# A hand-planned hybrid decoder layer: new order of the front units, new planner prices, new due times of the weight sums

## The chip, the core and the metric

The kernel runs on one core of a Trainium2 chip. Its engines are PE (TensorE: matmuls, transposes, and weight loads, which the profile lists as PEld), DVE (VectorE), ACT (ScalarE), POOL (GpSimd) and SP (SyncE, which issues nearly all DMAs here). Each engine works through its own queue in the order in which the program issued the instructions. The metric is the time of one execution in microseconds (us); lower is better.

## What is computed

One layer with two token mixers side by side on 1024 tokens of width 1024. All data is float32.

```python
h = rms_norm(x, norm_w)
proj = h @ w_in
q, k, v, z_a, xbc, z_s, dt_raw, gate_logits = jnp.split(proj, SPLIT_POINTS, axis=-1)
y_a = diff_attention(q, k, v, ...) * silu(z_a)          # 8 heads, two causal softmax maps each
xbc = silu(causal_depthwise_conv(xbc, conv_w, conv_b))
xs, Bm, Cm = jnp.split(xbc, ...)
y_s = ssd_chunked(xs, softplus(dt_raw + dt_bias), A, Bm, Cm, d_skip)   # 4 groups, chunks of 128 tokens
y_s = gated_group_rms_norm(y_s, z_s, ssd_norm_w)
g_a, g_s = jnp.split(gate_logits, 2, axis=-1)
merged = sigmoid(g_a) * (y_a @ w_proj_attn) + sigmoid(g_s) * (y_s @ w_proj_ssd)
x = x + merged @ w_out
```

## The kernel before

Every large product is made of matmuls on a high and a low part: a float32 operand is copied by ACT into the matmul's reduced format (the high part), and a subtract gives the low part (a "split"); three matmuls (high by high, high by low, low by high) make one block. Large products also use a seven-product scheme on 2 by 2 blocks: sums of blocks, called t1 to t4 ("forms") for the activations, and sums of weight blocks are made first, seven products p = 1 to 7 are run in place of eight, and DVE adds them up.

**The planner.** All instructions are written out by generators under a planner (class `Plan`). It keeps a clock `pl.t`, which moves with each PE instruction by a price, and a busy time for each other engine, which `act`, `tt`, `stt` and their like move by a price worked out from the size. A generator yields the planned time at which its next input will be ready. The planner always resumes whatever is due, so the prices and the due times decide in which order the instructions stand in each engine's queue. They decide nothing else: on the chip an instruction waits for semaphores, however late they come. [...]

**The front**, to about 580 us. `FRONT_ORDER` lists its units, and `bulk` runs them one after the other on PE:

- y0, y1 (`z_first`): plain z units, eight weights of 128x512 each, all of the first four token tiles; y0 starts while the tokens still come in and are normalised.
- e0, e2, e4, e6 (`gate_first`): half of a gate block row in two parts of 12 matmuls. The first part is copied out by ACT (`gc`) before the second part goes on in the same PSUM bank.
- c0 to c22 (`front_pair`): a pair of 128-column blocks of xBC in the seven-product scheme, seven products of 12 matmuls; each of its outputs then runs through the depthwise convolution and silu (`conv`, mostly on DVE).
- g0 to g10 (`front_pair`): the same for gates; those whose e unit came before need five products.
- z03 to z17 (`z_part`): one product p of the seven for z, 48 matmuls; the first digit is the half of the columns. Its weights are plain blocks or, for p = 3, 5, 6, 7, sums that `weight_sums` made.
- d0 (`dt_proj`): the dt projection; `dt_rest` then makes the scan's tables, mostly on DVE.

`form_evac` makes the forms of the second four tiles, t2 first, then t3, t1, t4. A weight set of a c or g unit is made by `pair_splits`: four additions on POOL, up to seven splits on ACT and DVE, some low halves on POOL. Raw weights have 4 buffers, split weights 9, both handed on in the order of the list `wlist`, which follows `FRONT_ORDER`; so the order of the units is also the order of the loads on SP.

**Behind the front** come eight heads (`att_proj` and the attention blocks), with the scan's 32 chunks spread between them (`ssd_core`), then four gate block rows (`gates`), the products with w_proj_ssd and w_proj_attn (`products`) and the last product (`final`). `ssd_core` waits `PACE` of planned time between chunks of a group, or `SLOW` = 32.0 while the front still holds its buffers.

**Weight sums.** `weight_sums(n, ...)` loads blocks of w_in (n = 0, 1) or w_out (n = 2), makes four sums of each four blocks on POOL (16 additions, 16 loads and 16 stores for each n) and stores them in `wf_d`, from which the z units and the last product load them. `ZSUMS` holds the due times. The first two are on the planner's clock; the third is an offset to the clock at the end of the heads.

**WPOOL, NEARLY.** In `w_splits` a 128x512 weight with index i in `wlist` has its low half made on POOL when i is at least `NEARLY`, a multiple of `WPOOL` and not one of the last product's; otherwise DVE makes it.

The prices that the change touches are in `mm`, `act`, `tt` and `stt` (the whole functions follow).

Of the kernel before, what the change touches and what calls it, by code (L numbers as in the profile page):

```python
# [30 lines left out]
C_ZS = 7168  # L31
C_DT = 9216
C_GATE = 9248
NBIG, NW, NRAW, NMID, NSM = 17, 9, 4, 16, 8
PACE = 19.5
FRONT = 12
SLOW = 32.0
FRONT_ORDER = "y0 e6 y1 e0 e4 c6 e2 d0 c20 z06 c16 z07 z05 g0 c2 z04 c0 z16 z03 g2 z17 z15 z14 c4 z13 c8 g8 c14 g6 c22 g10 c12 g4 c10 c18"
REST = (("t2", 6), ("b22", 3), ("t3", 7), ("t1", 5), ("t4", 4))
ZSUMS = (75.0, 182.0, 11.0)  # L40
WPOOL = 3
NEARLY = 48
FINAL = (("b11", 1), ("t1", 5), ("t2", 6), ("t3", 7), ("b21", 2), ("b22", 3), ("t4", 4))
NFIN = 4 * len(FINAL)
HOP = 0.12
# [100 lines left out]
def tile_hybrid_layer(ctx: ExitStack, tc: tile.TileContext, x, norm_w, w_in, q_norm_w, k_norm_w,  # L146
# [4 lines left out]
    w_in, w_pa, w_ps, w_o = w_in[0], w_proj_attn[0], w_proj_ssd[0], w_out[0]  # L151
# [24 lines left out]
    pl = Plan()  # L176
# [10 lines left out]
    def midt(shape=(P, 512), dt=F32, name="m"):  # L187
        return mid.tile(list(shape), dt, tag="b2", name=name)
# [16 lines left out]
    lag = [0.0135, 1.5]  # L205

    def mm(o, lhsT, rhs, start, stop, after=0.0, **kw):
        nc.tensor.matmul(o, lhsT=lhsT, rhs=rhs, start=start, stop=stop, **kw)  # L208
        n, m = rhs.free_size(), lhsT.free_size()
        if rhs.dtype == F32:  # L210
            c = max(4 * n / 2400, 0.215)
        else:
            c = max(n / 2400 + lag[0], 0.057 if m <= 64 else 0.107)
        pl.t = max(pl.t, after) + c

    def tp(o, i, idn=None, after=0.0):
# [11 lines left out]
    def in_ps(*aps):  # L228
        return any(a.space == bass.MemoryType.PSUM for a in aps)
# [3 lines left out]
    def act(o, i, f, after, **kw):  # L233
        nc.scalar.activation(o, i, f, **kw)  # L234
        if f in (AF.Silu, AF.Exp) and f != table[0]:
            table[0] = f
            pl.op("A", 1.3, after)
        c = 0.83e-3 * i.free_size() + (0.052 if in_ps(i) else 0.093) + 0.093 * (("accum_out" in kw) + any(not isinstance(kw.get(i, 0.0), float) for i in ("scale", "bias")))
        return pl.op("A", c, after)

    def tt(o, a, b, op, after, eng="V"):
        (nc.vector if eng == "V" else nc.gpsimd).tensor_tensor(out=o, in0=a, in1=b, op=op)  # L242
        n = o.free_size()
        if eng == "G":
            return pl.op("G", 0.095 + (1.85e-3 if op == ALU.mult else 2.3e-3) * n, after, True)
        sb = not in_ps(a, b)
        return pl.op("V", 0.07 + 0.07 * sb + 1.042e-3 * n, after, sb)

    def stt(o, a, s, b, op0, op1, after):
        nc.vector.scalar_tensor_tensor(out=o, in0=a, scalar=s, in1=b, op0=op0, op1=op1)  # L250
        sb = not in_ps(a, b)
        return pl.op("V", 0.07 + 0.07 * sb + 1.042e-3 * o.free_size() + (0.0 if isinstance(s, float) else 0.06), after, sb)

    def tsc(o, a, s, op, after):
        nc.vector.tensor_scalar(out=o, in0=a, scalar1=s, scalar2=None, op0=op)
# [6 lines left out]
    def load(o, i, after=0.0):  # L262
        nc.sync.dma_start(out=o, in_=i)
        q = pl.op("Q", 0.48, max(after, pl.t))
        n = o.free_size() * 512 / 360e3 if o.space != bass.MemoryType.DRAM else i.free_size() * 512 / 360e3
        return pl.op("D", n, q + 0.6) + lag[1]
# [32 lines left out]
    ready = {}  # L299
# [59 lines left out]
    ORDER1 = []  # L359
    for e in FRONT_ORDER.split():  # L360
        ORDER1.append((e[0], int(e[1:])))
# [88 lines left out]
    def w_splits():  # L450
        for i in range(len(wlist)):
# [20 lines left out]
            if i >= len(wlist) - NFIN:  # L472
                yield from pl.room("V", 2.0)
            t = tt(lo, raw, hi, ALU.subtract, t, "G" if NEARLY <= i < len(wlist) - NFIN and i % WPOOL == 0 else "V")
            raws.give(kr, t)
# [307 lines left out]
    def att_setup():  # L783
        ready['setup'] = 1
        for i in range(2):
            kqlo.append((yield from pl.get(bigs)))
            q = bigt([P, 2, 512], F32R, name=f"qlo{i}")
            nc.gpsimd.memset(q[64:P, 0].bitcast(F32), 0.0)
            nc.gpsimd.memset(q[0:64, 1].bitcast(F32), 0.0)
            qlo.append(q)  # L790
# [549 lines left out]
    def z_part(pr, p, keep):  # L1340
        f, ids = FORM_OF[p], w_next(4)
        for t in range(4):
            k = yield from pl.get(trs, first=True)
            pm = trt(f"pz{p}{pr}{t}")
            if f[0] == "t":
                yield from formed(f, (4 + t,))
            us = {}
            pl.spawn(z_fetch(pr, p, t, us))
            for kb in range(4):
                yield from w_need(ids[kb])  # L1350
                yield from steps3(pm, [a[:, t * P:(t + 1) * P] for a in front_form(f, kb)], wide(ids[kb]), kb == 0, kb == 3)
                if t == 3:
                    w_done(ids[kb])
            pl.spawn(z_step(pr, p, t, pm, k, us, keep), pe_done())
# [117 lines left out]
    def ssd_core(g):  # L1472
# [20 lines left out]
        for c in range(NT):  # L1493
# [4 lines left out]
            pl.spawn(ssd_chunk(g, c, state, abs_))  # L1498
            yield pl.t + (PACE if bigs.avail(3) <= pl.t or 'setup' in ready else SLOW)

# [179 lines left out]
    def gates():  # L1680
        for ob in range(FRONT, 16):
            ids = w_next(2)
            for n in range(2):
                k = yield from pl.get(trs, first=True)
                pm = mmt(f"pg{ob}{n}")
                yield from proj_half(pm, ids, n, n == 1, ob == 15 and n == 1)
                pl.spawn(gate_evac(ob, n, pm, k), pe_done())
# [21 lines left out]
    def prepare():  # L1709
        for c, g in ((0, 1), (1, 3)):  # L1710
            while ready.get("ssd", {}).get(g, INF) > pl.t:
                yield pl.t + 0.5
            yield from sums_of(c, range(4))
            if c == 0:
                pl.spawn(prepare_a())

    def weight_sums(n, src, c0, at=0.0):
        yield at
        for kb in range(4):
            ks = yield from pl.get(mids, 4)  # L1720
            a, b = [[midt(name=f"os{n}{kb}{j}{i}") for i in range(2)] for j in range(2)]
            t = max(load((a, b)[j][i], src[(j * 4 + kb) * P:(j * 4 + kb + 1) * P, c0 + i * 512:c0 + i * 512 + 512])
                    for j in range(2) for i in range(2))
            yield t
            for p, x, k, o, y, z, op in ((5, b[1], 3, b[1], b[1], a[1], ALU.add), (7, a[1], 1, a[1], a[0], a[1], ALU.subtract),
                                         (6, a[0], 0, a[0], b[1], a[0], ALU.subtract), (3, b[0], 2, b[0], b[0], a[0], ALU.subtract)):
                yield from pl.room("G")
                t = tt(o, y, z, op, t, "G")
                pl.spawn(sum_store(n, kb, p, x, ks[k], t))
                if p == 3:  # L1730
                    ready["summed", n, kb] = t
                t -= HOP

    def sum_store(n, kb, p, x, k, t):
        yield t
        j, h = {6: (0, 0), 7: (0, 1), 3: (1, 0), 5: (1, 1)}[p]
        ready[n, kb, p] = t = load(wf_d[n * 4 + kb, j][:, h * 512:(h + 1) * 512], x, t)
        while p == 6 and ("summed", n, kb) not in ready:
            yield pl.t + 0.2
        mids.give(k, max(t, ready["summed", n, kb]) if p == 6 else t)  # L1740
# [389 lines left out]
    def ssd_all():  # L2130
        for g in range(GROUPS):
            while "tables" not in ready:
                yield pl.t + 0.5
            yield from ssd_core(g)

    def bulk():
        pl.spawn(ssd_all())
        pl.spawn(prepare())
        step = {"y": z_first, "h": att_proj, "e": gate_first}
        for i in range(2):  # L2140
            pl.spawn(weight_sums(i, w_in, C_ZS + i * 1024, ZSUMS[i]))
        for n, (kind, i) in enumerate(ORDER1):
            if kind in PAIR_C:
                yield from front_pair(kind, i, (kind, i) == FPAIRS[-1])
            elif kind == "z":
                nk, ni = ORDER1[n + 1]
                yield from z_part(*divmod(i, 10), nk == "z" and ni // 10 == i // 10)
            elif kind in step:
                yield from step[kind](i)
            else:  # L2150
                yield from dt_proj() if kind == "d" else att_setup()
        pl.spawn(fill())
        pl.spawn(weight_sums(2, w_o, 0, pl.t + ZSUMS[2]))
        yield from gates()
        lag[:] = [0.0135, 2.5]
        for c in range(3):
            yield from products(c)
        yield from final()
# [38 lines left out]
    with tc.manual_schedule():  # L2197
        pl.spawn(start())
        pl.spawn(rest())
        pl.run(bulk())  # L2200
# [28 lines left out]
```

## Time and profile before

| what | value |
| --- | --- |
| three runs | 1579.36, 1580.61, 1582.21 us; median 1580.61 |
| the profiled execution | 1580.41 us, its span 1578.7 us |
| mean granted PE clock | 0.998 |
| heads' projection `pma` on PE | 581.3 to 1205.1 us |
| gate rows `pg` on PE | 1206.0 to 1264.6 us |
| DMA | 287.38 MB, mean 182 GB/s |

The span runs from the first to the last instruction of the profiled execution. The profile's page gives the busy time of each engine; the view of waits says for each engine how long it stood idle, and which instruction of which engine (or which DMA) ended that. Names are the program's own without buffer numbers: `fYc<-ft,wp` is a matmul into the bank fY of a c unit from a form and a split weight, `pz` a z unit, `pmz` a y unit, `pe` an e unit, `pO`, `px`, `py` banks of the scan (the last two also of the products), `pma` and `sc` a head's projection and scores. `L242` is line 242, the helper `tt`; as most instructions are issued by a helper, the tile's name says more than the line.

### The profile page before, as it was taken

How to read it: one execution, taken by the hardware profiler on the slowest of the kernel's cores; microseconds unless marked ns; L12 is line 12 of the kernel's file. 1: busy time of each engine (PE TensorE's matmuls, PEld its weight loads, DVE VectorE, ACT ScalarE, POOL GpSimd, SP SyncE). 2: the span in 40 equal slices, each digit the busy share in tenths (PEclk: the TensorE clock that was granted, in tenths of full speed). 3: DMA queues.
4: the chain of work that ended last, by engine and by line, in shares of the span. 5: the costliest groups of instructions: out<-in, count | busy, mean ns of one | idle time of the engine just before them, and what ended most of it. 6: DMA issues, size and time to landing. Idle time of an engine off the chain costs nothing.

```text
span 1578.7 us, 24834 instructions
## 1 busy us (share of the span) xinstructions
PE 1553.7 (98%) x7858; PEld 1299.0 (82%) x7858; DVE 1183.6 (75%) x2143; ACT 939.4 (60%) x2273; POOL 785.3 (50%) x906
## 2 busy tenths in 40 slices
PE   7999999999999999999999999999999999999999
PEld 5777888888888888888888888888888888888887
DVE  6778867568787778767778787877556687898985
ACT  7653434467565576778677777776666554443350
POOL 3274465345555554546574846454756745332005
PEclk9999999999999999999999999999999999999999
DMA  6576698744454552424373522333336697798846
GB/s 227 162 250 194 230 301 284 247 153 139 133 150 157 151 158 96 134 62 122 111 236 122 152 89 81 110 112 118 107 134 224 193 366 253 267 323 273 302 140 220
DMA packets 254821, 287.38 MB, mean 182 GB/s; under 512 B 18391, under 2 KB 162528, under 8 KB 254690
## 3 DMA queue, kind: packets, MB, share of 16 engines
q1 hardware_dynamic: 254686, 285.79, 55.7%
q8 instruction: 62, 1.02, 0.3%
q14 instruction: 69, 0.57, 0.1%
q10 hardware_dynamic: 4, 0.00, 0.0%
HBM read 196.47 MB, written 89.26 MB: 181 GB/s over the span
## 4 chain that ended last, share of the span: by engine, by line
PE 85%; ACT 3%; DVE 3%; DMA 3%; POOL 3%; issue 2%; SPq 0%; POOLq 0%; DVEq 0%; ACTq 0%
PE pma L208 19%; PE pz L208 11%; PE py L208 5%; PE fYc L208 5%; PE sc L208 4%; PE pO L208 4%; PE av L208 4%; PE fXc L208 3%; PE fZc L208 3%; PE px L208 3%; PE fYg L208 3%; PE pg L208 2%; PE pmz L208 2%; PE pa L217 2%; PE poz L208 1%
## 5 line engine op out<-in xcount | busy, mean ns | idle before, releaser
L208 PE MATMUL pma<-w,hH 128*128 128x512 f32 x1024 | 343.8, 404 | 0.0
L208 PEld LDWEIGHTS pma<-w,hH 128*128 128x128 f32 x1024 | 187.7, 189 | 32.9 <-DVE xdt L242 0.2
L208 PE MATMUL pma<-w,hL 128*128 128x512 f32 x512 | 205.7, 402 | 0.0
L234 ACT ACTIVATE w<-raw 128x512 fp32r<-128x512 f32 (+1 forms) x166 | 101.3, 629 | 56.0 <-DMA raw<-wf_d 21.7
L242 DVE TENSOR_TENSOR w<-raw,w 128x512 fp32r<-128x512 f32 (+1 forms) x134 | 107.1, 817 | 27.0 <-ACT w L234 24.1
L234 ACT ACTIVATE p<-p,nm 128x256 f32<-128x256 f32 (+7 forms) x128 | 98.8, 774 | 33.8 <-DVE nm L916 33.3
L208 PEld LDWEIGHTS pma<-w,hL 128*128 128x128 f32 x512 | 96.5, 188 | 16.6
L242 POOL TENSOR_TENSOR rawf<-rawf,rawf 128x512 f32<-128x512 f32 x54 | 71.8, 1330 | 75.1 <-DVE wp L242 30.5
L208 PE MATMUL fYc<-ft,wp 128*128 128x512 f32 x432 | 106.5, 392 | 2.4 <-DVE ft L242 1.8
L208 PEld LDWEIGHTS fYc<-ft,wp 128*128 128x128 f32 x432 | 80.3, 188 | 20.2 <-DVE ft L242 2.2
L208 PE MATMUL pz<-w,ft 128*128 128x512 f32 x384 | 90.1, 391 | 0.9 <-DVE w L242 0.9
L234 ACT ACTIVATE wp<-rawp 128x512 fp32r<-128x512 f32 x72 | 44.1, 627 | 78.4 <-POOL rawp L242 25.6
L242 POOL TENSOR_TENSOR os<-os,os 128x512 f32<-128x512 f32 x48 | 66.9, 1393 | 36.4 <-DMA os<-in_w_in_dram 14.8
L208 PEld LDWEIGHTS pz<-w,ft 128*128 128x128 f32 x384 | 71.7, 188 | 16.0 <-DVE w L242 1.3
L242 POOL TENSOR_TENSOR rawp<-rawp,rawp 128x512 f32<-128x512 f32 x36 | 54.4, 1521 | 54.2 <-DVE wp L242 50.2
L234 ACT ACTIVATE ab<-ab,nac 128x128 f32<-128x128 f32 x256 | 78.5, 397 | 3.5 <-POOL ab L1482 3.4
L916 DVE CUSTOM_DVE_ANT_0 p<-sc,maskb 128x512 f32<-128x512 f32 (+3 forms) x128 | 72.4, 584 | 6.6 <-PE sc L208 6.0
L274 POOL TENSOR_TENSOR rs<-rs,mhalf 128x4 f32<-128x4 f32 (+1 forms) x71 | 72.8, 1025 | 5.9
L208 PE MATMUL av<-v,at 128*128 128x128 f32 x576 | 75.2, 275 | 0.0
L208 PEld LDWEIGHTS av<-v,at 128*128 128x128 f32 x576 | 72.5, 191 | 3.2
L234 ACT ACTIVATE wp<-rawf 128x512 fp32r<-128x512 f32 x100 | 60.5, 624 | 17.5 <-POOL rawf L242 16.3
L948 POOL TENSOR_TENSOR rec<-s,mone 128x1 f32<-128x1 f32 x64 | 37.2, 583 | 63.7 <-ACT p L234 62.5
(376 smaller groups left out, 4410.3 us busy)
## 6 DMA issues: line engine op xcount, KB each, us to landing
raw<-in_w_in_dram SPq DMA_DIRECT2D x104, 256.0 KB, 3.2
rawf<-in_w_in_dram SPq DMA_DIRECT2D x72, 256.0 KB, 4.7
ab<-act_d SPq DMA_DIRECT2D x32, 512.0 KB, 4.7
wf_d<-os SPq DMA_DIRECT2D x48, 256.0 KB, 5.1
cv_d<-cv SPq DMA_DIRECT2D x48, 256.0 KB, 2.9
raw<-wf_d SPq DMA_DIRECT2D x48, 256.0 KB, 3.3
t_d<-ts SPq DMA_DIRECT2D x24, 512.0 KB, 4.0
os<-in_w_in_dram SPq DMA_DIRECT2D x32, 256.0 KB, 3.8
```

The costliest lines, as they stand in the source:

```text
L208: nc.tensor.matmul(o, lhsT=lhsT, rhs=rhs, start=start, stop=stop, **kw)
L217: nc.tensor.transpose(out=o, in_=i, identity=ident if idn is None else idn)
L234: nc.scalar.activation(o, i, f, **kw)
L242: (nc.vector if eng == "V" else nc.gpsimd).tensor_tensor(out=o, in0=a, in1=b, op=op)
L274: nc.gpsimd.tensor_tensor(out=dst, in0=dst, in1=mhalf[:, 0:cols], op=ALU.pow)
L916: nc.vector.tensor_tensor_reduce(out=p[:, j:e], in0=sc[i][:, 0:e - j], in1=maskb[:, S - n + j:S - n + e], scale=-1.0, scalar=nms[i - 1] if ...
L948: nc.gpsimd.tensor_tensor(out=rec, in0=sums[1], in1=mone, op=ALU.pow)
```

## The change

It changes the unit order, five constants and some planner prices, and spawns the third weight sums with the first two. No instruction of the computation is added or left out.

```diff
-PACE = 19.5
+PACE = 18.0
-FRONT_ORDER = "y0 e6 y1 e0 e4 c6 e2 d0 c20 z06 c16 z07 z05 g0 c2 z04 c0 z16 z03 g2 z17 z15 z14 c4 z13 c8 g8 c14 g6 c22 g10 c12 g4 c10 c18"
+FRONT_ORDER = "y0 y1 e6 e4 c6 e0 e2 d0 c4 c20 z06 c16 z07 z05 c22 c2 z03 z04 g0 z16 c0 g2 z17 z15 c12 g6 g8 g10 z14 c8 c14 z13 g4 c18 c10"
-ZSUMS = (75.0, 182.0, 11.0)
-WPOOL = 3
-NEARLY = 48
+ZSUMS = (75.0, 187.0, 1190.0)
+WPOOL = 4
+NEARLY = 57
...
-            c = max(n / 2400 + lag[0], 0.057 if m <= 64 else 0.107)
+            c = max(n / 2400 + lag[0], 0.057 if m <= 64 else 0.107) + (0.006 if 'setup' in ready and n == 512 and lag[1] < 2 else 0.0)
...
-        return pl.op("A", c, after)
+        return pl.op("A", c + part(o), after)
+
+    def part(o):
+        return 0.12 if o.shape[0] == 64 else 0.0
...
-        return pl.op("V", 0.07 + 0.07 * sb + 1.042e-3 * n, after, sb)
+        return pl.op("V", 0.065 + part(o) + 1.042e-3 * n, after, sb)
...
-        return pl.op("V", 0.07 + 0.07 * sb + 1.042e-3 * o.free_size() + (0.0 if isinstance(s, float) else 0.06), after, sb)
+        return pl.op("V", 0.065 + part(o) + 1.042e-3 * o.free_size() + (0.0 if isinstance(s, float) else 0.06), after, sb)
...
-        for i in range(2):
-            pl.spawn(weight_sums(i, w_in, C_ZS + i * 1024, ZSUMS[i]))
+        for i, (src, c0) in enumerate(((w_in, C_ZS), (w_in, C_ZS + 1024), (w_o, 0))):
+            pl.spawn(weight_sums(i, src, c0, ZSUMS[i]))
...
         pl.spawn(fill())
-        pl.spawn(weight_sums(2, w_o, 0, pl.t + ZSUMS[2]))
```

`'setup' in ready` holds from the end of the front on; `lag[1] < 2` holds until the gate rows are done. `sb` is true when no input lies in PSUM. `part` is for pieces of 64 partitions, which the heads' q and k stacking uses.

## The prediction

> **What bounds the kernel now.** I read the page first: which engine has no time left.
>
> ```profile
> span 1578.7 us, 24834 instructions
> PE 1553.7 (98%) x7858; PEld 1299.0 (82%) x7858; DVE 1183.6 (75%) x2143; ACT 939.4 (60%) x2273; POOL 785.3 (50%) x906
> ```
>
> PE (TensorE) is busy for 1553.7 of 1578.7 us, so PE's own work is the bound, and the change adds and removes none: it sorts the same units anew. All that can be won is idle time of PE, so the second view is the waits of engine PE alone (who ended the wait; us in total, times, longest).
>
> ```profile
> PE pmz L208 <- ACT zc L234: 4.3, 2, 2.9
> PE pe L208 <- ACT gc L234: 2.9, 4, 0.7
> PE nwb L208 <- POOL one L2164: 2.7, 1, 2.7
> PE fYc L208 <- DVE ft L242: 1.8, 1, 1.8
> PE ph L217 <- DVE x L250: 1.6, 1, 1.6
> PE pO L208 <- POOL wp L242: 1.4, 1, 1.4
> PE py L208 <- DVE u L242: 1.1, 1, 1.1
> PE fXc L208 <- ACT fc L234: 0.9, 1, 0.9
> PE pz L208 <- DVE w L242: 0.9, 1, 0.9
> PE fYg L208 <- DVE fu L242: 0.8, 1, 0.8
> PE fYc L208 <- DVE fu L242: 0.7, 1, 0.7
> PE pod L208 <- DVE xr L250: 0.6, 1, 0.6
> PE pa L217 <- DVE p L250: 0.4, 1, 0.4
> ...
> PE sc L208 <- DVE kk L242: 0.2, 1, 0.2
> ```
>
> The sum is some 22 us; the seven waits from `pa` to the last one are 0.2 to 0.4 each, 2.0 together. Third, the busy times by stage say where they lie (columns: PE, weight loads, DVE, ACT, POOL busy us, then clock, DMA share, GB/s).
>
> ```profile
> 40.00:160.00 120.00, 113.82 (x503) 89.12 (x502) 94.39 (x154) 61.15 (x124) 56.02 (x43) 1.00 0.63 200
> 160.00:440.00 280.00, 280.00 (x1291) 232.63 (x1290) 200.26 (x308) 147.43 (x280) 141.09 (x115) 1.00 0.67 215
> 440.00:580.00 140.00, 136.95 (x661) 113.83 (x660) 106.79 (x165) 85.91 (x170) 76.18 (x68) 1.00 0.48 146
> 580.00:1060.00 480.00, 478.23 (x2783) 411.84 (x2782) 367.78 (x817) 354.56 (x1053) 261.59 (x408) 1.00 0.39 121
> 1206.00:1300.00 94.00, 92.91 (x463) 77.35 (x462) 72.21 (x107) 57.02 (x123) 58.51 (x55) 1.00 0.86 290
> ```
>
> PE idles 6.2 us in 40 to 160 (the four `pe` waits, 1.8 of `ft`, 0.9 of `pz`, 0.7 of `fYc`), nothing in 160 to 440, 3.1 in 440 to 580 (`pO`, `fXc`, `fYg`), 1.8 in 580 to 1060 and 1.1 in 1206 to 1300 (`py`). The front is nearly full already.
>
> **What the change cannot reach.** `nwb` 2.7, `ph` 1.6 and `pmz` 4.3 lie before 40 us, where y0 runs as before; `pod` 0.6 is the last store. The `pe` waits, 2.9, are inside each of the four e units: its second half waits for the copy of its first, and there are still four. The 0.7 of `fYc` follows d0, behind which a c unit still stands. Together 12.8. Left are 1.8 + 1.4 + 1.1 + 0.9 + 0.9 + 0.8 = 6.9, and the 2.0 of the small ones.
>
> **Part 1, the order of the front.** First y1 directly behind y0. Its supply decides (chain of waits and DVE's timeline):
>
> ```profile
> 46.99 2.73 PE pe L208 x12
> 53.41 21.76 PE pmz L208 x96
> 50.90 0.69 DVE L242 TENSOR_TENSOR w<-raw,w 128x512 fp32r<-128x512 f32 x1 [0.89 <-ACT w L234]
> 103.93 2.35 PE L208 MATMUL fYc<-ft,wp 128*128 128x512 f32 x9 [1.76 <-DVE ft L242]
> 102.78 1.42 DVE L242 TENSOR_TENSOR ft<-r,ft 128x256 fp32r<-128x256 f32 x4
> 85.48 2.56 ACT L234 ACTIVATE ft<-r 128x256 fp32r<-128x256 f32 x8
> ```
>
> y1 would start at 47.0 in place of 53.4. Its eight loads pass e6's two on SP's queue, and its splits on ACT and DVE pass them too. With e6's two splits behind them y1's last two move up by two places, and I read the row at 50.90 as the place of the last. PE uses that weight after half of the first tile pair (21.76 / 4 = 5.4) and three blocks of 0.7, near 54.5. No wait, cost 0; were it late, 0.7 for each split that it is late by.
>
> c6 then starts at 47.0 + 21.8 + two e units of 6.4 (53.41 - 46.99) = 81.6, 6.4 us sooner than behind three e units. Its wait of 1.8 is for the form t4: ACT had it copied by 88.0 (85.48 + 2.56), but DVE wrote the low halves in pieces, the last from 102.8 to 104.2. c6 now needs t4 at 103.93 - 1.76 - 6.4 = 95.8. With the pieces done right behind ACT's copy it is ready near 90 and 1.8 goes; if they stay where they are, 6.4 more are lost. I take the first, by the ACT row, which is nearer to the data. `pz` 0.9: the only z unit in 40 to 160 is z06, and it waits for a split on DVE, where I read c20's convolutions in front of it; they run late because d0's table chain shares DVE. Now c4 stands between d0 and c20, so I take it as gone (0 to -0.9). Sum: -2.7.
>
> In 440 to 580 all three waits fall in one unbroken run of ten c and g units (c8 to c18). The new order cuts it by z14 and z13 into runs of four, two and three; but c4 c20 and c22 c2 now touch where the old order had z units. Of the 3.1 I take half, -1.5 (0 to -3.1), and for the new joints one wait of the mean size, 6.9 / 6 = +1.2 (0 to +1.4 at each of the two: +2.8).
>
> **Part 2, the planner's prices.** They move no instruction by themselves, but the planner sorts every queue by them.
>
> ```profile
> 57.88 1.29 DVE L242 TENSOR_TENSOR b<-b,r 128x512 f32<-128x512 f32 x2
> 59.09 1.28 DVE L242 TENSOR_TENSOR r<-b,r 128x512 f32<-128x512 f32 x2
> 622.14 1.41 DVE L242 TENSOR_TENSOR kk<-pq,kk 64x512 fp32r<-64x512 f32 x2
> 182.75 1.90 SPq L263 DMA_DIRECT2D os<-in_w_in_dram  x4
> ```
>
> Two DVE operations with both inputs in SBUF start 59.09 - 57.88 = 1.21 us after the pair before, 0.60 each. The old price is 0.14 + 0.53 = 0.67, the new one 0.60: right. A half-height `kk` takes 1.41 - 0.69 = 0.72; the old price is 0.60, the new one 0.72: right. The second weight sums, due at 182.0 of the planner's clock, left SP at 182.75: in the front that clock holds already, so a better order in the plan should be one on the chip. In the heads I give the corrected prices 0.5 of the 2.0 small waits (0 to -2.0; as much the other way, since the old 0.07 was also a margin).
>
> [...]
>
> ```profile
> L242 DVE TENSOR_TENSOR w<-raw,w 128x512 fp32r<-128x512 f32 x132 | 106.6, 825 | 27.0 <-ACT w L234 24.1 <-POOL xn L242 1.3 <-issue 1.2
> L242 DVE TENSOR_TENSOR hL<-ph,hH 128x512 fp32r<-128x512 f32 x16 | 10.5, 684 | 4.5 <-ACT b L234 4.5
> L242 POOL TENSOR_TENSOR w<-raw,w x32: 1275/1294/1837, 249.1 to 1213.1; 128x512 fp32r<-128x512 f32 x32
> ```
>
> With both inputs in SBUF the same shape takes 825 ns on the mean, with one in PSUM 684. [...]
>
> **Part 3, WPOOL and NEARLY.** Every fourth weight from 57 on, not every third from 48, has its low half made on POOL. By the list's order that is 20 (indices 60, 64, 72, 80 and sixteen of the heads'), 12 fewer than the 32 of the row: POOL loses 12 x 1.3 = 16 us, DVE gains 12 x 0.83 = 10. DVE is 77% busy in the heads (367.78 of 480), so other work of PE hides it: 0 (up to +0.4, one small wait).
>
> **Part 4, PACE 18.0 and the third sums.**
>
> ```profile
> L1482 POOL TENSOR_SCALAR_AFFINE_SELECT ab<-ab x32: 1090/1098/1555, 294.6 to 1064.4; 128x1024 f32<-128x1024 f32 x32
> L208 PE MATMUL pma<-w,hH 128*128 128x512 f32 x1024 | 343.8, 404 | 0.0
> L208 PE MATMUL pma<-w,hL 128*128 128x512 f32 x512 | 205.7, 402 | 0.0
> 1214.39 3.51 SPq L263 DMA_DIRECT2D os<-in_w_out_dram  x4
> 1277.04 5.11 DMA wf_d<-os
> ```
>
> The scan's 32 chunks run from 294.6 to 1064.4, the later ones paced. In the front they are 32 apart, so nine start before 580 and 23 behind it; with 1.5 less for each the scan ends about 35 us sooner, but PE is full there and DVE at 77%: 0 (up to +0.4 for each chunk whose work DVE then does late, one small wait, 9 in all). The extra 0.006 us for each of 1536 matmuls puts the planner's clock 9.2 us later at the end of the heads. The w_out sums were due 11 after that end and left SP at 1214.39; due at 1190 they leave between 0 and 24 us sooner, with 16 loads, 16 stores and 16 additions, past the gate weights on SP and among the last heads' small POOL work. The `py` wait, 1.1, stands at the end of the busiest DMA stretch (share 0.86), whose chain holds such a store: half goes, -0.5 (-1.1 to +0.4).
>
> **The sum.** -2.7 - 1.5 + 1.2 - 0.5 - 0.5 = -4.0. The profiled execution took 1580.4 (1.7 outside the span), the median of the three is 1580.6, so one sum serves both: 1580.4 - 4.0 = **1576.4**.
>
> **Rivals.** *The waits only change places.* Each of the six comes back at a new joint: 1580.4. For it: the front already has 280 us without one, so any new order risks more there than it can win. Against: every wait has its own cause above, and the new order touches most. *Nearly all of it goes*: 6.9 of waits and some of the 2.0: 1580.4 - 7.5 = 1573. For it: the clock of the plan holds at 182. Against: three of the waits were in an order that the same planner made. *Slower: POOL behind c4 and c20.* c4 and c20 now run while POOL makes the first w_in sums; a pair's weight set that misses its turn costs the 1.4 of `pO <- POOL wp`. From six of the 14 sets on (6 x 1.4 = 8.4 against 1576.4) the kernel ends at 1584.8, slower. Against: POOL is 47% busy in 40 to 160 (56.02 of 120) and gets one pair more.
>
> **Chances.** Forecast (1574.5 to 1578.5) 0.45; nearly all goes 0.17; waits change places (1578.5 to 1583.8) 0.23; slower 0.15. About 0.2%, 3.2 us, is what a measurement of this kernel can tell from no change. Faster than 1577.4: three quarters of the forecast and the second case, 0.51; slower than 1583.8: 0.15; between: 0.34. For eight in ten the range goes from 1572 (the second case and a little) to 1584 (the third case whole).
>
> **What would show it.** In the waits of PE: `fYc <- ft` and `pz <- w` gone; `pe <- gc` four times 0.7; the three of 440 to 580 halved. y1 behind y0 without a wait, c6 from about 81. If c6 waits for `ft` by more than 2 us, or new waits on `wp` stand between 120 and 160, part 1 is wrong; if the waits of 580 to 1060 grow beyond 4 us, parts 2 to 4 are.

## The result: 1595.5 us, slower, and the profile after

The changed kernel takes 1595.52 us (median of four runs, 1595.29 to 1596.22) beside 1580.59 of the kernel before (median of four): the ratio is 1.0095, with a 95% interval from 1.0077 to 1.0112. It is 15 us slower where 4 us less were forecast, and outside the range. The profiled execution took 1596.22 us.

The page after, its span and the busy times of the engines:

```profile
span 1594.5 us, 24858 instructions
PE 1560.8 (98%) x7858; PEld 1300.1 (82%) x7858; DVE 1196.2 (75%) x2153; ACT 934.8 (59%) x2269; POOL 772.5 (48%) x896
```

PE has the same 7858 instructions. It idles 33.7 us (before 25.0), and it is busy 7.1 us longer for the same work, so some matmuls run slower; 8.7 and 7.1 make the 15.8 us by which the span has grown. The waits of PE after:

```profile
PE fYg L208 <- DVE fu L245: 4.7, 3, 3.0
PE pmz L208 <- ACT zc L234: 4.3, 2, 2.9
PE pO L208 <- ACT yt L234: 3.6, 1, 3.6
PE pe L208 <- ACT gc L234: 2.9, 4, 0.7
PE nwb L208 <- POOL one L2166: 2.7, 1, 2.7
PE pya L217 <- DVE y L253: 2.2, 2, 1.6
PE pa L217 <- ACT yt L234: 1.7, 1, 1.7
PE ph L217 <- DVE x L253: 1.5, 1, 1.5
PE pa L217 <- DVE y L253: 1.3, 1, 1.3
PE py L217 <- ACT xn L234: 1.0, 2, 0.8
PE sc L208 <- DVE kk L245: 0.9, 1, 0.9
PE pa L217 <- ACT at L234: 0.7, 1, 0.7
```

The waits called out of reach (`pmz`, `pe`, `nwb`, `ph`) are there to within a tenth. `fYc` on `ft`, `pz` on `w`, `pO` on `wp`, `fXc` on `fc` and `py` on `u` are gone. `fYg` on `fu` has grown from 0.8 to 4.7, and new, or longer than before, is a row of waits on `yt`, `y`, `kk` and `at`. The busy times by stage say where (columns as before):

```profile
40.00:160.00 120.00, 117.06 (x516) 91.98 (x517) 97.26 (x149) 63.68 (x128) 61.86 (x46) 1.00 0.58 184
160.00:440.00 280.00, 275.77 (x1237) 227.38 (x1236) 201.16 (x310) 132.19 (x247) 131.63 (x104) 0.99 0.68 218
440.00:580.00 140.00, 138.44 (x662) 114.44 (x662) 104.12 (x169) 90.29 (x180) 70.52 (x64) 1.00 0.58 176
580.00:1060.00 480.00, 470.94 (x2731) 402.54 (x2730) 359.95 (x789) 344.32 (x1018) 253.82 (x391) 1.00 0.38 116
1206.00:1300.00 94.00, 90.75 (x462) 75.29 (x461) 72.95 (x105) 58.20 (x141) 65.10 (x67) 1.00 0.76 265
```

Idle time of PE falls from 6.2 to 2.9 us in 40 to 160 and from 3.1 to 1.6 in 440 to 580: there the change does what was forecast. It rises from 0 to 4.2 in 160 to 440, from 1.8 to 9.1 in 580 to 1060, and from 1.1 to 3.2 in 1206 to 1300. In 160 to 440 the mean clock is also below 1.00. Two stretches make the difference:

```profile
283.10:290.00 6.90, 6.09 (x14) 4.79 (x15) 2.55 (x4) 0.00 (x0) 2.55 (x2) 0.51 0.60 174
870.20:873.60 3.40, 3.40 (x10) 2.62 (x9) 1.01 (x2) 1.53 (x4) 0.66 (x2) 0.50 0.54 169
```

In these 10.3 us the granted clock was half; in the trace of the kernel before every 2 us between 31 and 1575 us has a mean clock of 1.00. By my estimate (half of 10.3, less the idle part) they are some 5 of the 7.1 us that PE is busy longer. Both stand at a long wait, and these come next.

**The place in 160 to 440** is the unit g0. Its third product waits for the sum `fu` (PE's timeline):

```profile
280.54 0.39 PE L208 MATMUL fXg<-hH,wp 128*128 128x512 f32 x1
283.91 5.46 PE L208 MATMUL fYg<-ft,wp 128*128 128x512 f32 x12 [2.99 <-DVE fu L245]
```

Twelve matmuls that take 2.88 to 3.00 us elsewhere in this trace (292 to 440) take 5.46 behind the wait, at a clock of 0.51. The place costs 3.0 and some 2.5 us.

**The longest wait in the heads** is `pO <- yt`. ACT's timeline shows what the small `yt` stood behind, and PE's what waited for it:

```profile
864.31 2.44 ACT L234 ACTIVATE ab<-ab,nac 128x128 f32<-128x128 f32 x8
866.65 2.76 ACT L234 ACTIVATE qh<-pq,cols 64x512 fp32r<-64x512 f32 x4
869.43 0.37 ACT L234 ACTIVATE yt<-pya,cols 128x128 f32<-128x128 f32 x1
...
869.85 0.50 PE L208 MATMUL pO<-sh,ch 128*128 128x512 f32 x1 [3.55 <-ACT yt L234]
```

`pO` doesn't use `yt` at all. It is a product of the scan; `yt` reads `pya`, a transpose of the attention. What they share is a PSUM bank: in the compiled program `pO` was given the bank that `pya` had. That became the main theory.

To compare kernels whose stages have different lengths, I also sum over each stage what every PE instruction takes from its start to the next start, less the median of its shape: the time that PE **loses**. The stages end at the first `pdt`, at the first and the last `pma`, at the last `pg`, and at the end. The first stage, up to `pdt`, scatters by 4 us among the runs of kernels whose order there is the same; it is left out. Each row is one profiled execution; the one of a_slot took 1590.53 us, the longest of its five.

| time lost by PE, us | front behind d0 | heads | gates | rest | sum |
| --- | --- | --- | --- | --- | --- |
| before | 7.9 | 12.4 | 0.9 | 2.3 | 23.5 |
| after | 12.4 | 22.4 | 4.7 | 0.9 | 40.4 |
| after, planner's banks (a_slot) | 12.0 | 15.3 | 3.8 | 1.0 | 32.1 |
| after, w_out sums as before (a_third) | 10.7 | 23.6 | 0.9 | 3.0 | 38.2 |
| after, second sums due at 190 (a_zs190) | 6.4 | 21.7 | 0.7 | 4.1 | 32.9 |
| after, banks and w_out sums (a_slotthird) | 10.8 | 15.3 | 0.9 | 2.9 | 29.9 |
| after, all three (a_zsslot3) | 6.9 | 17.6 | 0.8 | 3.2 | 28.5 |
| after, banks and c0 moved up (a_slotc0) | 11.0 | 15.8 | 3.8 | 0.7 | 31.3 |

### The profile page after: what moved, and what is told of

It reads as the page before. It is cut to its first block, busy times and chain, and to the rows that moved or that the text cites. A ratio compares the mean times of both kernels' runs of the same rounds, so it can differ in the third digit from the quotient of the medians.

```text
span 1594.5 us, 24858 instructions
## 1 busy us (share of the span) xinstructions
PE 1560.8 (98%) x7858; PEld 1300.1 (82%) x7858; DVE 1196.2 (75%) x2153; ACT 934.8 (59%) x2269; POOL 772.5 (48%) x896
## 4 chain that ended last, share of the span: by engine, by line
PE 78%; DVE 6%; ACT 5%; DMA 5%; issue 3%; POOL 1%; SPq 1%; DVEq 0%; ACTq 0%; POOLq 0%
PE pma L208 19%; PE pz L208 8%; PE py L208 6%; PE fYc L208 5%; PE pO L208 4%; PE px L208 4%; PE av L208 3%; PE sc L208 3%; PE fXc L208 3%; PE fZc L208 3%; PE fYg L208 3%; PE pmz L208 2%; PE pa L217 2%; PE fZg L208 1%; PE poy L208 1%
## 5 line engine op out<-in xcount | busy, mean ns | idle before, releaser
L245 DVE TENSOR_TENSOR w<-raw,w 128x512 fp32r<-128x512 f32 (+1 forms) x144 | 120.5, 850 | 16.7 <-ACT w L234 16.0
L208 PE MATMUL sc<-kk,qh 128*128 128x512 f32 (+3 forms) x192 | 66.1, 349 | 0.9 <-DVE kk L245 0.9
```

## Experiments

Every time stands beside runs of the kernel before on the same chip; the ratio is to those, with its 95% interval. Differences in us are ratios times 1581.

### Banks

The planner's `Slots` hands out the bank that comes free first on its clock. The program does not know this choice: `ps_tr` gives a new tile a free bank by its own order. In the changed kernel's compiled program 865 of 897 tiles got, of the banks free at that point of the program, the one whose last reader stands first in it (864 of 897 in the kernel before). `yt` had been issued early, behind a long queue on ACT; so its bank was handed on early although it came free late. The experiment gives each tile the bank that the planner chose. The order of the instructions on every engine stays the same.

```diff
-    def trt(name):
-        return ps_tr.tile([P, 512], F32, tag="tr", name=name)
+    def trt(name, k):
+        return ps_tr.tile([P, 512], F32, tag=f"tr{k}", name=name, bufs=1)
...
-            pO = trt(f"pO{g}{c}")
+            pO = trt(f"pO{g}{c}", k)
```

> The changed kernel, with every PSUM tile put into the bank that the planner's clock chose for it; the order of the instructions on every engine is the same. Theory 1 (banks): in the heads PE waits because the next tile gets the bank whose last reader was issued first, not the one that came free first; of the waits of 580 to 1060 some 8.9 us are of that kind (pa on y 1.4, pa on yt 1.9, pa on at 0.8, pO on yt 3.7), so they go and the time is 7 to 9 us shorter, near 1587.5. Rival (queues): ACT and DVE are late as such under the new pace and prices, and PE waits for their data; then the time stays within 2 us of 1595.5 and the waits come back on data.

Measured: 1586.57 us, 1.0037 (1.0024 to 1.0050); the changed kernel has 1.0095, so 9 us are gone. The waits of PE from 580 to 1206 (there were 9.1 us in eight such rows):

```profile
PE pa L217 <- DVE y L253: 1.3, 1, 1.3
PE py L217 <- ACT xn L234: 0.9, 2, 0.7
PE px L217 <- DVE qlo L253: 0.5, 1, 0.5
PE pa L217 <- DVE p L253: 0.5, 1, 0.5
PE pma L208 <- DVE qk L245: 0.2, 1, 0.2
```

The waits on `yt` and `at` are gone, and the sum fell to 3.4 us; the wait on `y` stays, because there the planner hands on the bank of the same tile. This settles it: ACT was not late as such. Theory 1 holds for most of the heads.

The same edit in the kernel before:

> The kernel before with its PSUM tiles in the planner's banks. Theory 1: only 1.9 us of its waits in the heads are handed-on banks, so 1 to 2 us shorter, 1579. Rival (queues): no change, 1580.6.

Measured: 1583.55 us, 1.0010 (1.0000 to 1.0021). No gain, where theory 1 asked for 1 to 2 us: the waits of 580 to 1206 sum to 1.8 us in the trace, before to 2.0, and short waits came elsewhere (0.6 us of `ph` at 42, 0.7 of `px` at 298). Putting the banks right gains only where the hand-out had gone wrong.

### What holds g0

The load of `fc`, which `fu` needs, left SP at 277.5 behind stores of z04. First it was issued from ACT's queue.

```diff
-            cell["ct"] = load(cell["c"], gc_d[b * P:(b + 1) * P], g_c[kind, b])
+            cell["ct"] = load(cell["c"], gc_d[b * P:(b + 1) * P], g_c[kind, b], nc.scalar)
```

> The changed kernel with the loads of fc (four of them, at g0, g2, g4, g6) issued from ACT's queue in place of SP's; nothing else is moved. Theory 1 (g0 behind z04): the 3.15 us at 280.5 come from that load, issued at 277.5 behind z04's stores on SP's queue, and another 2.7 us from the matmuls at 0.43 us behind the wait; both go, and half of the 2.1 us at g2 and g4: 6 to 7 us shorter, 1589. Rival: DVE's own queue is late at 283; then the wait moves to the next thing and less than 1.5 us go.

Measured: 1596.92 us, 1.0102 (1.0089 to 1.0115). Nothing gained; the load left at 270.1 and the wait was still 3.25:

```profile
281.54 4.57 PE L208 MATMUL fYg<-ft,wp 128*128 128x512 f32 x12 [3.25 <-DVE fu L245]
```

The theory of the load falls here, the rival holds: on DVE `fu` stood right behind weight splits that were late themselves.

```profile
279.44 1.35 DVE L245 TENSOR_TENSOR w<-raw,w 128x512 fp32r<-128x512 f32 x2 [1.26 <-ACT w L234]
280.72 0.68 DVE L245 TENSOR_TENSOR fu<-fc,fYg 128x512 f32<-128x512 f32 x1
```

> Both edits in the changed kernel. If they are independent, the gains add: 13 to 16 us shorter, 1580 to 1582, level with the kernel before; if the planner's promise holds (its clock, in the old prices, ends 7.7 us before that of the kernel before), as far as 1575.

Measured: 1589.07 us, 1.0051 (1.0037 to 1.0064). No gain over the banks alone. In its profile g0's wait was 1.5 us and the slow matmuls were missing (twelve took 3.00), but that was one execution; the times say nothing of it.

The late splits wait for raw weights from `wf_d`, which stood on SP behind stores of z units. So the stores that ACT's own results need went to ACT's queue: `z_d` alone, then `cv_d`, `gt_d` and `gc_d` as well.

```diff
-        at = load(z_d[g, t * P:(t + 1) * P, :], zz, at)
+        at = load(z_d[g, t * P:(t + 1) * P, :], zz, at, nc.scalar)
```

> The changed kernel with its PSUM tiles in the planner's banks (1586.6) and, besides, the z_d stores issued from ACT's queue, which writes zu, in place of SP's. Theory 1b (g0): the load of fc was not the cause, DVE is held by weight splits whose raw loads from wf_d leave SP at 273 to 277, behind z_d stores that wait 5.1 us for ACT; without these stores on SP the raw loads leave some 4 us sooner, the 2.4 us at g0 and the 1.7 us of slow matmuls behind it go: 4 us shorter, 1582.5. Rival: the DMA engines are full there (the share is 0.9 from 262 to 284), the loads come no sooner, and less than 1.5 us go.

> As the run with z_d, and the stores of cv_d, gt_d and gc_d, which ACT writes too, go by ACT's queue as well. Theory 1b: SP waits 76.8 us for cv and 19.5 for fu in the changed kernel; without these its loads run ahead and the waits at g2 and g4 shrink too: 5 to 7 us shorter than with banks alone, 1580 to 1582. Rival (DMA full): as with z_d alone, less than 1.5 us.

> The same four kinds of store by ACT's queue in the kernel before, its banks as they were. Its front has 11 us of waits on data, of which fYg and fXc on fu and fc, pO on wp, pz on w some 5 us could be late loads: 1 to 3 us shorter, 1578; if SP's queue costs nothing there, 1580.6.

Measured: 1588.40 us, 1.0047 (1.0035 to 1.0060); 1595.00, 1.0080 (1.0066 to 1.0093); 1581.66, 0.9999 (0.9990 to 1.0008). No gain, a loss of 7 us, and no difference. In the profile of the first g0's wait was still 3.14 us: SP waiting in its queue for these stores is not what holds g0. If the bytes themselves were (DMA share 0.95 in 260 to 280), half of two kinds of store should show it. This kernel leaves out half of z and of the convolutions:

```diff
-        at = load(z_d[g, t * P:(t + 1) * P, :], zz, at)
+        nc.sync.dma_start(out=z_d[g, t * P:t * P + 64, :], in_=zz[0:64])
...
+    def load2(o, i):
+        nc.sync.dma_start(out=o[0:64], in_=i[0:64])
+        nc.sync.dma_start(out=o[64:128], in_=i[0:64])
...
-        t_z = load(zc, z_d[g, cs, :])
+        t_z = load2(zc, z_d[g, cs, :])
```

> The changed kernel with its PSUM tiles in the planner's banks (1586.6), and half the bytes of two kinds of store: only 64 of the 128 rows of each tile of z_d and cv_d are stored, and the scan reads these rows twice (so half of the gate z and of the convolutions is left out of what is computed). In 220 to 285 this takes 17 stores x 128 KB, some 2.2 MB, 7 us of DMA at the 0.32 MB/us of 260 to 280. Theory 1c (the DMA engines are full before g0, share 0.95): the weights come sooner, the wait of 2.4 to 3.3 us for fu at 283 and the slow matmuls behind it go, and some of the 3 us at 520: 4 to 7 us shorter, 1580 to 1582. Rival (the order of a queue, not the bytes): the wait stays above 2 us, 1586.

Measured: 1591.48 us, 1.0063 (1.0050 to 1.0076), more than with banks alone. g0's wait was 1.58 us in its profile, less but not gone; the scan's four extra loads for each chunk may have taken the rest back. It leans to the bytes and settles nothing.

Then one constant, the due time of the second w_in sums, which the change had set from 182 to 187:

```diff
-ZSUMS = (75.0, 187.0, 1190.0)
+ZSUMS = (75.0, 190.0, 1190.0)
```

> The changed kernel with one constant moved: the second w_in sums due at 190 in place of 187. My prediction treated such a due time as worth nothing by itself: 1595.5. Theory 3 (the plan is a greedy sort that jumps; the change's constants sit on one of its low points): the planner's clock ends 13.1 us later: 1605 to 1609.

Measured: 1587.40 us, 1.0038 (1.0025 to 1.0052): 9 us shorter, where the planner's clock said 13 longer and my prediction nothing. g0 has no wait, twelve of its matmuls take 3.00 us, and the mean clock of the profiled execution is 0.998, as before the change, where the changed kernel has 0.996:

```profile
278.87 0.39 PE L208 MATMUL fXg<-hH,wp 128*128 128x512 f32 x1
279.36 3.00 PE L208 MATMUL fYg<-ft,wp 128*128 128x512 f32 x12
```

SP's queue shows what goes with it. With 187 the last four loads of these sums leave at 244.8, and all that follows leaves late:

```profile
244.82 1.85 SPq L266 DMA_DIRECT2D os<-in_w_in_dram  x4
...
256.93 2.23 SPq L266 DMA_DIRECT2D rawf<-in_w_in_dram  x4
...
273.10 0.38 SPq L266 DMA_DIRECT2D raw<-wf_d  x1
```

With 190 the sums' last loads leave earlier, and g0's weights with them:

```profile
239.14 1.94 SPq L266 DMA_DIRECT2D os<-in_w_in_dram  x4
...
252.59 2.23 SPq L266 DMA_DIRECT2D rawf<-in_w_in_dram  x4
...
267.47 0.37 SPq L266 DMA_DIRECT2D raw<-wf_d  x1
```

A later due time let the loads run earlier: the planner's sort put the sums at another place among the other loads. In the table the front loses 6.4 us in place of 12.4, less than before the change.

### The w_out sums

Their due time alone, back behind the end of the heads; all up to 1190 stays.

```diff
-        for i, (src, c0) in enumerate(((w_in, C_ZS), (w_in, C_ZS + 1024), (w_o, 0))):
-            pl.spawn(weight_sums(i, src, c0, ZSUMS[i]))
+        for i in range(2):
+            pl.spawn(weight_sums(i, w_in, C_ZS + i * 1024, ZSUMS[i]))
...
+        pl.spawn(weight_sums(2, w_o, 0, pl.t + 11.0))
```

> The changed kernel with the third weight sums (w_out) spawned as before, 11 us behind the end of the heads; everything up to 1190 is the same. My prediction: the new due time is worth 0.5 us (py 1.1), so 1596. Theory 2: the earlier loads crowd DVE and the DMA engines in 1206 to 1300, whose waits grew from 1.3 to 3.6: then 2 us shorter, 1593.5. By the planner's clock it ends 3.6 us later: 1599.

Measured: 1590.92 us, 1.0062 (1.0047 to 1.0077), some 5 us shorter. From 1206 to 1300 PE has no waits left:

```profile
1206.00:1300.00 94.00, 93.89 (x479) 78.87 (x478) 68.80 (x106) 59.82 (x139) 63.90 (x65) 1.00 0.80 272
```

By the table the gates gain 3.8 and the rest gives 2.1 back; the whole sum falls by 2.2, the time by 5, so I take 2 to 5. Theory 2 has the sign right.

### Do they add up?

The edits above together: the due time of 190 with the banks, the w_out sums with the banks, and all three.

> The changed kernel with the second w_in sums due at 190 and the PSUM tiles in the planner's banks. If the causes add: 5.3 us of handed-on banks are left in the heads with 190, so 4 to 5 us shorter than the 1587.4 of 190 alone: 1582.5 to 1583.5. Rival: with 190 the sort of the heads is another one and the banks cost nothing there: 1587.

> The changed kernel with the planner's banks and the w_out sums due as before. If the causes add: 1586.6 less the 5 us that the due time gave by itself: 1581 to 1583. Rival: the 1590.9 of the due time alone was a chip's difference: 1586.

> All three. With 190 the gates wait only 0.6 us, so the third due time has little left to give: 0 to 2 us below the run with 190 and banks, 1581 to 1583, level with the kernel before; then the loss is accounted for. If it stays above 1586, something else holds part of it.

Measured: 1586.24 us, 1.0029 (1.0018 to 1.0041); 1585.17, 1.0020 (1.0011 to 1.0028); 1586.38, 1.0028 (1.0016 to 1.0040). They don't add: each alone gave 9, 9 and 5, all three together 10.5 of the 15, and the banks with the w_out sums 12; the intervals of the three overlap. With 190 the heads are sorted differently and lose 17.6 to 18.7 even with the planner's banks. About 4 us are in none of the three. By the table they are in the heads: 17.6 against 12.4.

### The parts alone in the kernel before, and the start of the scan

The change's own `FRONT_ORDER` line alone; its edits of `mm`, `act`, `tt` and `stt` alone; and the due time that helped the changed kernel:

```diff
-ZSUMS = (75.0, 182.0, 11.0)
+ZSUMS = (75.0, 190.0, 11.0)
```

> The kernel before with the new FRONT_ORDER alone. My prediction priced the parts one by one from waits of before, the order alone at -3.0: 1577.6. Rival (the parts belong together): with the other constants as before the planner's clock ends 24.6 us later than with the old order, so the plan itself has that idle time: near 1605.

> The kernel before with the new prices alone (part 2). My prediction: -0.5 us, 1580. Theory 3: the planner's clock ends 25.7 us later, of which some 12 are the 0.006 us that each 512-column matmul costs on the chip in any case: 12 to 18 us longer, 1592 to 1598.

> The kernel before with its second w_in sums due at 190 in place of 182. The planner's clock ends 18.5 us later. If the chip follows the planner: 1597 to 1600. If the chip goes its own way, as with 187 to 190 in the changed kernel (planner 13.1 later, chip 8 sooner): within 6 us of 1581.

Measured: 1601.57 us, 1.0126 (1.0111 to 1.0140); 1594.58, 1.0087 (1.0072 to 1.0103); 1596.72, 1.0095 (1.0082 to 1.0108). So 20, 14 and 15 us slower, near what the planner's clock says (24.6, 25.7 less the 12.3 of the new matmul price, 18.5). Of that price's 0.006 us for a 512-column matmul the trace of before shows 0.004: the heads' `pma` matmuls start 231 ns apart on the median, the front's 227. The parts cannot be priced one by one. The clearest row is the new order with the old prices: c6 waits for its form, which it does not when the new prices come along.

```profile
PE pe L208 <- ACT gc L234: 4.6, 4, 2.3
...
PE fZc L208 <- DVE ft L242: 3.0, 1, 3.0
```

What my prediction had wholly missed is when the scan starts. It needs c16, c20, c0, c2 and all of z's first group; the new order puts c0 behind g0 and z16. The scan's transposes (first and last start) before:

```profile
L217 PE MATMUL px<-ident,xr x128: 270/272/328, 296.4 to 1052.2; 128*128 128x128 f32 x128
```

And after:

```profile
L217 PE MATMUL px<-ident,xr x128: 270/272/299, 353.6 to 1087.9; 128*128 128x128 f32 x128
```

It starts 57 us later and ends 36 later, and seven chunks in place of nine lie ahead of the heads. Two runs test whether that is the loss:

```diff
-            while "tables" not in ready:
+            while "tables" not in ready or pl.t < 340.0:
```

```diff
-FRONT_ORDER = "... z05 c22 c2 z03 z04 g0 z16 c0 g2 ..."
-ZSUMS = (75.0, 187.0, 1190.0)
+FRONT_ORDER = "... z05 c22 c0 c2 z03 z04 g0 z16 g2 ..."
+ZSUMS = (75.0, 182.0, 1190.0)
```

> The kernel before with one thing added: the scan may not begin before 340 of the planner's clock (it begins at 296 otherwise, in the changed kernel at 354). My prediction had no such term: 1581. Theory 4 (late scan): one or two chunks more fall into the heads, whose idle time and slow matmuls grow from 12.4 by 6 to 12 us, and the time grows by 10 to 20 us: 1591 to 1601 (by the planner's clock by 25).

> The changed kernel with the planner's banks, the second sums due at 182 as before, and c0 moved from behind z16 to ahead of z03, so that the scan's last input comes some 45 us sooner; PACE stays 18. Theory 4: nine chunks lie ahead of the heads again, the heads lose 12 to 13 us as before and last some 625 in place of 636; the front gets 8.7 us of PE work back: 1579 to 1583. By the planner's clock it ends 5.3 us later than the changed kernel: 1592. Rival: the heads lose 15 us or more whenever the scan begins.

Measured: 1597.67 us, 1.0111 (1.0094 to 1.0128), and 1587.17, 1.0037 (1.0023 to 1.0051). Held back, the scan does cost the kernel before 17 us, in the size forecast, but not where: the heads lose 15.1 in place of 12.4, the front 15.6 in place of 7.9, and behind the gates PE waits 4.8 for the first form of the next product:

```profile
PE pz L208 <- ACT f0b L234: 4.8, 1, 4.8
```

In the changed kernel the early scan (309 to 1032 us, nine chunks ahead) gains nothing over the banks alone, and the heads still lose 15.8, as theory 4's rival said. The test is not clean: the run moves the sums' due time too, and a new wait of 3.9 us (`pO` on `ab`, at 485) stands in it. That the shorter `PACE` makes up for the late start there would fit, but no run shows it. What the heads lose beyond before, 3 to 5 us, stays open. `PACE` and `WPOOL` with `NEARLY` were not tried by themselves.

No run is clearly faster than the kernel before; the nearest, b_actq, is level with it.

## Why the prediction was wrong, step by step

- **The fixed 12.8 us**: right for `nwb`, `ph`, `pmz` and `pe`; the 0.7 of `fYc` and the 0.6 of `pod` went as well.
- **Part 1, the front's waits**: right where it named a wait. y1 stands behind y0 without one, `ft` and `pz` went (-3.3 us in 40 to 160, forecast -2.7), and c6 runs from 81.5 (forecast 81.6). 440 to 580 gave -1.5, as forecast, but not as described: `pO` and `fXc` went whole, `fYg` grew from 0.8 to 1.2, and 0.3 of `px` is new, so the number is partly luck.
- **Part 1, "for the new joints one wait of the mean size, +1.2"**: mis-sized, and put at c4 c20 and c22 c2. The joint that failed was z04 to g0: a wait of 3.0 plus 2.5 of slow matmuls. A wait was priced at its own length; that the clock would be 0.51 behind one of 2.99 us was in no term. With the second sums due at 190 in place of 187 the wait is gone; the text didn't price that due time.
- **Part 2, "in the front that clock holds already, so a better order in the plan should be one on the chip"**: the step that failed most. The row at 182.75 was a single one: in the changed kernel the sums due at 187 left SP at 189.1, and those due at 190 at 187.9. And the planner's clock speaks only of what it models. It does not model which bank the program hands out, and in the changed kernel that cost some 9 us (waits of 580 to 1060: 9.1, where 0.5 less than 1.8 was forecast). The prices were right for the rows shown; that did not make the plan true. Put into the kernel before by themselves, the new prices cost 14 us (forecast -0.5) and the new order 20 (forecast -3.0): pricing each part from waits of the old trace failed, since either one sorts every queue anew.
- **Part 3**: 0 was forecast; not tested by itself. Its count of 20 weights on POOL was low by two: the trace after has 22.
- **Part 4, "the scan ends about 35 us sooner"**: wrong; it ends 36 later, since the start was read from the trace of before although Part 1 moved c0. In the kernel before a start held back to 349 cost 17 us, so a late scan can be dear; what it costs in the changed kernel stays open.
- **Part 4, the w_out sums, -0.5**: `py` did go, but the earlier loads held up DVE in the gates (0.9 on `kk`, 2.2 on `y`): 2 to 5 us lost, the wrong sign.
- **The rivals**: "waits change places" came nearest, with far too small a price, that of the six old waits; the new waits have other causes. The slower case named POOL behind c4 and c20; PE waits 0.7 for `wp` in all, so it did not happen. The line on what would show parts 2 to 4 wrong (waits beyond 4 us in 580 to 1060) was the right place to look.

The planner's clock explains why the change looked good. It ends at 1566.1; of that 12.3 are the new 0.006 us of 2049 matmuls, so in the old prices near 1554, against 1561.5 before. With one of its constants moved (due times, `PACE`, `WPOOL`, `NEARLY`), the planner's clock ended at 1569.3 to 1588.7 in 21 settings, never lower: the change sits at a low point of a jagged plan. On the chip its neighbour at 190 is 9 us faster. The kernel before looks like such a low point too: of four edits to it (new order, new prices, 190, 340) each ends later in the plan, and there the chip follows, with 14 to 20 us. That the argument was true before made it no argument for another low point.

## What to carry over

A schedule chosen by a model's clock is only as good as what the model leaves out; compare plan and trace for the candidate itself, and where the plan picks a resource (a bank, a buffer), make the program use that choice. When PE waits on an instruction whose result it does not need, look at who had its buffer before. When parts of a change set one greedy sort, price them together or not at all, and follow each moved unit to everything that starts when it ends.

## What was not expected of the hardware

At g0 the wait did not only cost its length. Behind 2.99 us twelve matmuls took 5.46 us at a clock of 0.51; in a_zs190, without the wait, they took 3.00. The same place in two other runs, a_slot and a_slotzq:

```profile
285.93 4.21 PE L208 MATMUL fYg<-ft,wp 128*128 128x512 f32 x12 [2.22 <-DVE fu L245]
...
283.90 3.00 PE L208 MATMUL fYg<-ft,wp 128*128 128x512 f32 x12 [3.14 <-DVE fu L245]
```

Behind 2.22 us twelve matmuls took 4.21 us, behind 3.14 us they took 3.00: in these runs the length of the wait alone does not decide it. In a_slot the clock fell only 1.5 us after the matmuls had begun again, and it stayed at half for 3.4 us:

```profile
285.93:287.40 1.47, 1.47 (x7) 1.23 (x8) 1.24 (x2) 0.00 (x0) 0.00 (x0) 0.99 0.99 292
287.40:290.80 3.40, 3.40 (x10) 2.64 (x9) 0.63 (x1) 0.00 (x0) 1.89 (x2) 0.50 0.41 117
```

What decides it, no run here shows.
